# A macaron layer in split float32: a fourth seven-product pair and a fourth DMA-made second part in every feed-forward group, and the final x turned during the last products

## The chip, the cores and the metric

The kernel runs on one core of one Trainium2 chip. The metric is the device time of one execution in microseconds; lower is better.

## The reference

One layer on x (256 tokens of 2048 features) with a memory of 256 tokens: a half-weighted SwiGLU feed-forward, a mixer of a convolution branch and a spatially gated branch, cross-attention into the memory with four heads, a second half-weighted SwiGLU feed-forward, and a last normalisation over features. The two feed-forwards are what the change touches:

```python
D_MODEL = 2048; SEQ = 256; D_FF = 5632

def swiglu_ffn(h, w_in, w_out):
    gate, up = jnp.split(h @ w_in, 2, axis=-1)
    return (jax.nn.silu(gate) * up) @ w_out

h = rms_norm(x, ffn1_norm);  x = x + 0.5 * swiglu_ffn(h, ffn1_w_in, ffn1_w_out)
...                                    # mixers, cross-attention
h = rms_norm(x, ffn2_norm);  x = x + 0.5 * swiglu_ffn(h, ffn2_w_in, ffn2_w_out)
return rms_norm(x, final_norm)
```

All inputs are float32, and the precision of float32 is kept by splitting every operand into two parts (below).

## The kernel before

**Products in two parts.** TensorE multiplies in a type with fewer bits than float32 (`F32R`). Each weight tile of 128 x 1024 is therefore split into a first part (ScalarE casts it, L341 in the feed-forward's first layer and L112 elsewhere) and a second part, what the cast left out (VectorE subtracts, L342 and L113). x is split likewise. A product is three matmuls: first by first, first by second, second by first. Weights stream from HBM on SyncE's queue, 512 KB a tile, each read once.

**The first layer of a feed-forward** (class `FeedForward`) runs over 11 groups of 512 hidden features. A group's weights are 2048 rows (16 tiles of 128, index k) by 1024 columns (512 gate, 512 up). Group 0 is done plainly in `run`. Groups 1 to 10 are done by `group`, which takes the 16 tiles as 8 pairs p (k = 2p and 2p+1) after a pattern of letters:

- `C` (`eight`): two tiles of 12 matmuls each, 24 in all (`by_two`, L288 to L291: L288 is first by first, L289 reads the weight's second part, L291 reads the first part again). Work besides: a cast and a subtraction for each tile.
- `S` (`seven`): the pair, both halves of the tokens and both of the columns are taken as a 2 x 2 block matrix, and seven products of sums stand for eight, 21 matmuls in all (`three`, L275 to L277). Work besides: four additions of 128 x 512 on VectorE (L387, L388, L393, L400), three casts and subtractions of 128 x 1024 and one of 128 x 512. The sums of x that it needs (`sides`) are made once, during group 0.

After the last `S` pair VectorE combines four accumulators (L439 to L442), after the last `C` pair it adds the rest (L452), and ScalarE and VectorE make the hidden features (L417, L419).

**Second parts by DMA** (`summed`, L354 to L359). For the tiles listed in `SUMMED`, all in `C` pairs, VectorE does not subtract. ScalarE writes the negated cast into the second half of the buffer `hl_s` (L357) and the cast into the first half (L358), and GpSimd's queue then issues a DMA that adds the raw tile onto the negated half (L359). There is one buffer `hl_s`. So a turnaround is: the last matmul that reads its second part (an L289), then L357, then the DMA of L359, then the first L289 of the next summed tile. The raw tile stays held until the DMA has read it.

**Order.** A scheduling layer sets the order of each engine's instructions at build time by its own costs; on the chip each engine then runs its list in that order, waiting on semaphores. Parts go through five buffers in turn (three `hl`, two `ring`), raw tiles through four buffers `raw` and a few pieces of the tile `spare`. In the first feed-forward those pieces are five (nine raw buffers in all). In the second the first 4096 columns of `spare` hold `x2`, the final x with tokens on partitions; 32 pieces of work (`turn`, L978, one transpose of 32 x 512 each) fill it, spread by `put` and `beside` over group 0 and the groups after. Until `x_turned` in group 3 there is one extra piece of `spare` (five raw buffers); then the tile `xT` is given up for four more (`raws`).

**The second layer** (`gemm_n`, L160 to L177): four blocks of 512 columns, 22 steps of two weight tiles each, 24 matmuls a step. After a block `add_up` adds it to `x2`.

Of the kernel before, what the change touches and what calls it, by code (L numbers as in the profile page):

```python
# [11 lines left out]
F32 = mybir.dt.float32  # L12
# [5 lines left out]
P = 128  # L18
D = 2048
# [16 lines left out]

PATTERNS = ("SCSCSCCC", "SCSCSCCC")

SUMMED = (2, 7, 13)

# [26 lines left out]
def layer(ctx: ExitStack, tc: tile.TileContext, a: dict):  # L67
    nc = tc.nc
    out = a["out"]
# [18 lines left out]
    def put(cost, *parts):  # L88

        later.extend((cost, p) for p in parts)  # L90
# [9 lines left out]
    def finish():  # L100
        while later:
            later.popleft()[1]()
# [196 lines left out]
    class FeedForward:  # L299
# [6 lines left out]
        def __init__(self, stack, tags, x_hl, gain, w_in, pattern):  # L306
# [18 lines left out]
            self.sums = spare[:, 4096:5120]  # L325
            self.raws = [spare[:, 5120:6144]]
            if tags[0] == "S1":
                self.raws += [spare[:, i * 1024:(i + 1) * 1024] for i in range(4)]
            self.raw_at = 0
# [92 lines left out]

        def group(self, j, r, per, after=()):
            b = {}
# [9 lines left out]
            for p, c in enumerate(self.pattern):  # L434
# [8 lines left out]
                else:  # L443
                    late = p > self.spairs[-1] and len(after) > 0
                    self.eight(j, p, b, p == self.pattern.index("C"), p == n - 1, late)
                    if p > self.spairs[-1] + 1:
                        for _ in range(2):
                            if after:
                                after.pop(0)()
                beside(per)  # L450
            for acc, u in (("2", p1), ("4", u2), ("3", u4), ("8", u5)):
                nc.vector.tensor_tensor(out=u, in0=u, in1=b[acc], op=ALU.add)  # L452
            self.give(j, (p1, u2), (u4, u5), r)

        def run(self, before, after, root, then, per):
            acc = token_accs()
# [13 lines left out]
            for j in range(1, NG):  # L470
                if j == 3:
                    then()
                if j < NG - 1:
                    self.group(j, r, per)
                else:
                    now, turns = turns[:4], turns[4:]
                    self.group(j, r, per, now)
            return turns
# [46 lines left out]
    with ExitStack() as stack:  # L525
# [21 lines left out]

        turns = ff.run(x_arrives, x_more, x_root, lambda: None, 0.0)

# [419 lines left out]
    with ExitStack() as stack:  # L969
        ff = FeedForward(stack, ("S0", "S1", "S2"), x_hl, "ffn2_norm", a["ffn2_w_in"], PATTERNS[1])  # L970
        x2 = ff.x2

        def turn(i, j):

            def go():
                q = j % 4
                dst = x2[32 * q:32 * q + 32, j // 4].rearrange("p (f n) -> p f n", n=P)
                nc.vector.transpose(  # L978
                    out=dst[:, :, 32 * i:32 * i + 32], in_=xT[32 * i:32 * i + 32, :, 32 * j:32 * j + 32]
                )  # L980
            return go

        h = ff.of
        put(0.6, *[turn(i, j) for i in range(4) for j in range(8)])

        def first_beside(k):
            if k in (6, 9, 12):
# [51 lines left out]
        for n in range(3):  # L1039
            acc = gemm_n(a["ffn2_w_out"][n], h) if n else acc_0  # L1040
            for t in range(2):
                add_up(t, slice(n * 512, (n + 1) * 512), acc[t], n)


# [92 lines left out]
```

## Time and profile before

| what | value |
|---|---|
| time, median of 3 runs | 2136.71 us (2135.22 to 2139.54) |
| the profiled execution's own time | 2133.17 us |
| its span, first to last instruction | 2131.4 us |
| TensorE busy | 2091.1 us (98%), 9764 matmuls |
| VectorE busy | 1559.3 us (73%) |
| ScalarE busy | 1153.5 us (54%) |
| DMA read from HBM | 405.99 MB |

TensorE's busy share is modelled at the ends of matmuls, so what counts is the idle time between matmuls and who ended it. A "summed" DMA is one issued at L359. Windows below are us from the start of the span: groups 1 to 10 of the first feed-forward run from about 54 to 437, the second's from about 1435 to 1874.

### The profile page before, as it was taken

Reading aid. Unit: us, or ns where it says so; the run is one execution under the profiler, and the core shown is the slowest. Engines: PE = TensorE matmul, PEld = TensorE weight load, DVE = VectorE, ACT = ScalarE, POOL = GpSimd, SP = SyncE. Lnnn points to the kernel's source line nnn. Section 1 sums busy time; section 2 is a strip of 40 time slices with the busy share of each in tenths; the row PEclk is TensorE's granted clock in tenths of the full one; section 3 lists DMA queues with packets and bytes.
Section 4 is the critical chain, followed back from the end, with each engine's and each line's share of the span. In section 5 each row is a group of like instructions: output and inputs, shape, how many; then the busy total and the mean of one; then the engine's idle time right before and its main releaser. Section 6 shows DMA issues by size and latency. Waiting matters only on the chain. (4 is left out here: it accounts for less than half of the span.)

```text
span 2131.4 us, 26548 instructions
## 1 busy us (share of the span) xinstructions
PE 2091.1 (98%) x9764; PEld 1739.2 (82%) x9764; DVE 1559.3 (73%) x2119; ACT 1153.5 (54%) x1450; POOL 63.9 (3%) x81
## 2 busy tenths in 40 slices
PE   8999999999999999999999999998999999999998
PEld 6887888888888888888888888886788778888886
DVE  6887888776655589888877666797777888765444
ACT  7655566555544454445754455554565566554443
POOL 0000000000000000000000000000000000000000
PEclk9999999999999999999999999999999999999999
DMA  9787778855766766666655544566788778656664
GB/s 349 218 240 227 240 236 242 254 159 169 220 191 188 222 223 201 180 186 180 187 193 185 185 153 129 192 201 195 238 242 236 232 233 257 188 157 203 191 194 149
DMA packets 121954, 440.23 MB, mean 207 GB/s; under 512 B 13664, under 2 KB 13792, under 8 KB 121696
## 3 DMA queue, kind: packets, MB, share of 16 engines
q1 hardware_dynamic: 113184, 407.35, 59.6%
q0 software_dynamic: 8352, 30.41, 7.7%
q8 instruction: 76, 1.25, 0.2%
q10 hardware_dynamic: 288, 0.79, 0.1%
q14 instruction: 54, 0.44, 0.1%
HBM read 405.99 MB, written 2.10 MB: 191 GB/s over the span
## 5 line engine op out<-in xcount | busy, mean ns | idle before, releaser
L113 DVE TENSOR_TENSOR hl<-raw,hl 128x1024 fp32r<-128x1024 f32 (+1 forms) x402 | 489.8, 1219 | 322.1 <-ACT hl L112 321.2
L112 ACT CAST hl<-raw 128x1024 fp32r<-128x1024 f32 (+1 forms) x402 | 419.5, 1045 | 485.9 <-PE acc L173 299.7
L288 PE MATMUL acc<-hl,x_hl 128*128 128x512 f32 x440 | 151.6, 395 | 15.1 <-ACT hl L341 15.1
L341 ACT CAST hl<-spare 128x1024 fp32r<-128x1024 f32 (+1 forms) x105 | 102.8, 999 | 107.5 <-DVE spare L388 69.3
L342 DVE TENSOR_TENSOR hl<-raw,hl 128x1024 fp32r<-128x1024 f32 (+1 forms) x115 | 130.2, 1137 | 40.1 <-ACT hl L341 39.7
L289 PE MATMUL acc<-hl,x_hl 128*128 128x512 f32 x440 | 158.3, 395 | 0.1
L341 ACT CAST hl<-raw 128x1024 fp32r<-128x1024 f32 (+1 forms) x115 | 111.3, 981 | 71.6 <-DVE raw L400 40.8
L291 PE MATMUL acc<-hl,x_hl 128*128 128x512 f32 x440 | 137.9, 393 | 0.0
L342 DVE TENSOR_TENSOR hl<-spare,hl 128x1024 fp32r<-128x1024 f32 (+1 forms) x105 | 120.7, 1159 | 21.2 <-ACT hl L341 21.0
L341 ACT CAST ring<-spare 128x1024 fp32r<-128x1024 f32 (+1 forms) x75 | 74.1, 996 | 68.7 <-DVE spare L388 43.5
L288 PEld LDWEIGHTS acc<-hl,x_hl 128*128 128x128 f32 x440 | 83.5, 191 | 33.2 <-ACT hl L341 15.9
L172 PE MATMUL acc<-hl,x_hl 128*128 128x512 f32 x256 | 100.5, 392 | 0.1
L172 PE MATMUL acc<-hl,m_hl 128*128 128x512 f32 x256 | 100.3, 392 | 0.0
L173 PE MATMUL acc<-hl,m_hl 128*128 128x512 f32 x256 | 100.2, 391 | 0.0
L173 PE MATMUL acc<-hl,x_hl 128*128 128x512 f32 x256 | 99.8, 390 | 0.0
L289 PEld LDWEIGHTS acc<-hl,x_hl 128*128 128x128 f32 x440 | 83.3, 190 | 18.6 <-DVE hl L342 1.5
L291 PEld LDWEIGHTS acc<-hl,x_hl 128*128 128x128 f32 x440 | 83.7, 190 | 17.7
L342 DVE TENSOR_TENSOR ring<-spare,ring 128x1024 fp32r<-128x1024 f32 (+1 forms) x75 | 86.3, 1156 | 11.4 <-ACT ring L341 11.4
L289 PE MATMUL acc<-ring,x_hl 128*128 128x512 f32 x256 | 92.0, 390 | 2.1 <-DVE ring L342 2.1
L289 PE MATMUL acc<-hl_s,x_hl 128*128 128x512 f32 x232 | 89.3, 390 | 2.2 <-DMA hl_s<-raw 1.7
L171 PE MATMUL acc<-hl,m_hl 128*128 128x512 f32 x256 | 91.2, 392 | 0.0
L125 PE MATMUL acc<-x_hl,hl 128*128 128x512 f32 x256 | 91.0, 398 | 0.0
(343 smaller groups left out, 5185.4 us busy)
## 6 DMA issues: line engine op xcount, KB each, us to landing
raw<-in_ffn_w_in SPq DMA_DIRECT2D x176, 512.0 KB, 4.8
raw<-in_ffn_w_out SPq DMA_DIRECT2D x176, 512.0 KB, 3.8
spare<-in_ffn_w_in SPq DMA_DIRECT2D x120, 512.0 KB, 5.1
raws<-in_ffn_w_in SPq DMA_DIRECT2D x56, 512.0 KB, 5.1
raw<-in_w_mix_vg SPq DMA_DIRECT2D x32, 512.0 KB, 4.6
raw<-in_w_k SPq DMA_DIRECT2D x32, 512.0 KB, 3.9
raw<-in_w_v SPq DMA_DIRECT2D x32, 512.0 KB, 4.3
raw<-in_w_mix_out SPq DMA_DIRECT2D x32, 512.0 KB, 3.8
```

Source lines behind the costliest of these rows:

```text
L112: nc.scalar.copy(out=hl[:, 0, :size], in_=raw[:, :size])
L113: newest[0] = nc.vector.tensor_tensor(out=hl[:, 1, :size], in0=raw[:, :size], in1=hl[:, 0, :size].bitcast(F32), op=ALU.subtract)
L125: nc.tensor.matmul(acc, lhsT=w_hi, rhs=x_hl, start=first, stop=False, skip_group_check=True)
L171: nc.tensor.matmul(acc[t], lhsT=x[:, 0, s], rhs=hi[:, k], start=k0 + k == 0, stop=False)
L172: nc.tensor.matmul(acc[t], lhsT=x[:, 0, s], rhs=lo[:, k], start=False, stop=False)
L173: nc.tensor.matmul(acc[t], lhsT=x[:, 1, s], rhs=hi[:, k], start=False, stop=k0 + k == nk - 1)
L288: nc.tensor.matmul(acc[t][g], lhsT=x[:, 0, s], rhs=hi[:, cols[g]], start=(t, g) in first, stop=False)
L289: nc.tensor.matmul(acc[t][g], lhsT=x[:, 0, s], rhs=lo[:, cols[g]], start=False, stop=False)
L291: nc.tensor.matmul(acc[t][g], lhsT=x[:, 1, s], rhs=hi[:, cols[g]], start=False, stop=last)
L341: nc.scalar.copy(out=hl[:, 0, :n], in_=raw[:, :n])
L342: newest[0] = nc.vector.tensor_tensor(out=hl[:, 1, :n], in0=raw[:, :n], in1=hl[:, 0, :n].bitcast(F32), op=ALU.subtract)
```

## The change

Three things are changed.

1. The pattern of both feed-forwards becomes `SCSCSSCC`: four `S` pairs of 8 a group, two of them (p = 4 and 5) next to each other. `sides` makes a fourth set of sums, at k = 15 of group 0.
2. `SUMMED` becomes (2, 6, 12, 15): four tiles a group have their second part made by DMA. The buffer `hl_s` stays one.
3. The 32 transposes of the final x leave the second feed-forward's groups. They become 128 transposes of 32 x 128 (L973), 32 of them beside block 0 of the last products and 96 beside blocks 1 and 2. `xT` is kept to the end, and both feed-forwards have nine raw buffers from the start, five of them in `spare`.

```diff
-PATTERNS = ("SCSCSCCC", "SCSCSCCC")
-
-SUMMED = (2, 7, 13)
+PATTERNS = ("SCSCSSCC", "SCSCSSCC")
+
+SUMMED = (2, 6, 12, 15)
...
-            self.raws = [spare[:, 5120:6144]]
-            if tags[0] == "S1":
-                self.raws += [spare[:, i * 1024:(i + 1) * 1024] for i in range(4)]
+            self.raws = [spare[:, i * 1024:(i + 1) * 1024] for i in (5, 0, 1, 2, 3)]
...
-                    if p > self.spairs[-1] + 1:
+                    if p >= n - 2:
...
-                beside(per)
...
-                if j == 3:
-                    then()
...
-            if k in (6, 9, 12):
+            if k in (6, 9, 12, 15):
                 ff.sides(k // 3 - 2)
-            beside(0.8)
-
-        def x_turned():
-            finish()
-            raws = xt.tile([P, 4, 1024], F32, name="raws", tag="x")
-            ff.raws += [raws[:, i] for i in range(4)]
-
-        turns = ff.run(lambda k: None, first_beside, lambda: rms_cols(ss, D, "r_x2"), x_turned, 0.6)
+        turns = ff.run(lambda k: None, first_beside, lambda: rms_cols(ss, D, "r_x2"))
+        put(0.3, *[turn(0, i, j) for i in range(4) for j in range(8)])
+        acc_0 = gemm_n(a["ffn2_w_out"][0], h, per=0.55, between=turns, after=0)
         finish()
-        acc_0 = gemm_n(a["ffn2_w_out"][0], h, between=turns, after=0)
...
         for n in range(3):
-            acc = gemm_n(a["ffn2_w_out"][n], h) if n else acc_0
+            if n == 1:
+                put(0.3, *[turn(m, i, j) for m in range(1, 4) for i in range(4) for j in range(8)])
+            acc = gemm_n(a["ffn2_w_out"][n], h, per=0.75) if n else acc_0
```

The lines above keep their meaning in the changed kernel but move: L357 and L359 become L355 and L357, L341 and L342 become L339 and L340; L275 to L291 stay.

**Where the order changes: TensorE around the summed tiles.** The names in a row are accumulator, weights and x, and what it waits for; the landing of a summed DMA is awaited as `DMASW`. Before, ahead of one of a group's three summed tiles in the first feed-forward. The second part of the summed tile before it was read for the last time 43 matmuls earlier; these are the last rows of that stretch:

```order
L277 MATMUL acc<-ring 128x512
L275 MATMUL aux<-hl,ring 128x512 [waits Activation_49]
L276 MATMUL aux<-hl,ring 128x512 [waits DVE_49]
L277 MATMUL aux<-hl,ring 128x512
L275 MATMUL acc<-hl,x_hl 128x512 [waits DVE_49,Activation_49]
L276 MATMUL acc<-hl,x_hl 128x512
L277 MATMUL acc<-hl,x_hl 128x512
L288 MATMUL acc<-hl_s,x_hl 128x512 [waits Activation_49]
L289 MATMUL acc<-hl_s,x_hl 128x512 [waits DMASW6_49]
```

Now, between a group's tile 15 and the next group's tile 2. The first row shown is the fifth matmul after the last that reads the second part of tile 15; the last row reads that of tile 2:

```order
L276 MATMUL acc<-ring,x_hl 128x512
L277 MATMUL acc<-ring,x_hl 128x512
L275 MATMUL acc<-ring 128x512 [waits DVE_49]
L276 MATMUL acc<-ring 128x512
L277 MATMUL acc<-ring 128x512
L275 MATMUL acc<-ring,x_hl 128x512 [waits DVE_49,Activation_49]
L276 MATMUL acc<-ring,x_hl 128x512
L277 MATMUL acc<-ring,x_hl 128x512
L288 MATMUL acc<-hl_s,x_hl 128x512 [waits Activation_49]
L288 MATMUL acc<-hl_s,x_hl 128x512 x2
L288 MATMUL acc<-hl_s,x_hl 128x512 [waits DVE_49]
L289 MATMUL acc<-hl_s,x_hl 128x512 [waits DMASW0_49]
```

So this turnaround has 16 matmuls from the start of one L289 to the start of the other, where the one before had 43. Over both feed-forwards the order before has 56 turnarounds, none under 34 matmuls and most of 43 to 61. The changed order has 76; 36 of them have 16 to 28 matmuls, 20.6 on average (tile 12 to 15, and 15 to the next 2), and the other 40 have 30 to 45.

**ScalarE, first feed-forward.** Before, between two negated casts:

```order
L357 ACTIVATE hl_s<-spare 128x1024 [waits DMAHW0_49,DMASW6_49,PE_49]
L358 CAST hl_s<-spare 128x1024 [waits PE_49,Activation_49]
L341 CAST hl<-raw 128x512 [waits DVE_49,Activation_49]
L341 CAST ring<-raw 128x1024 [waits DMAHW5_49,PE_49,Activation_49]
L341 CAST ring<-spare 128x1024 [waits PE_49,Activation_49]
L341 CAST hl<-raw 128x1024 [waits DMAHW0_49,PE_49,Activation_49]
L341 CAST hl<-spare 128x1024 [waits DMAHW7_49,PE_49,Activation_49]
L341 CAST hl<-spare 128x512 [waits DVE_49,PE_49,Activation_49]
L341 CAST ring<-spare 128x1024 [waits DMAHW1_49,PE_49,Activation_49]
L357 ACTIVATE hl_s<-raw 128x1024 [waits DMAHW6_49,DMASW7_49,PE_49]
```

Now, three negated casts (for tiles 15, 2 and 6) within twelve rows:

```order
L355 ACTIVATE hl_s<-spare 128x1024 [waits DMASW2_49,PE_49]
L356 CAST hl_s<-spare 128x1024 [waits PE_49]
L339 CAST hl<-spare 128x1024 [waits DMAHW3_49,PE_49]
L339 CAST ring<-raw 128x512 [waits DVE_49]
L355 ACTIVATE hl_s<-raw 128x1024 [waits DMAHW5_49,DMASW3_49,PE_49]
L415 ACTIVATE h_109<-spare,r_x_95 128x512 [waits DVE_49]
L356 CAST hl_s<-raw 128x1024 [waits PE_49,Activation_49]
L415 ACTIVATE h_109<-spare,r_x_95 128x512 [waits DVE_49]
L339 CAST ring<-spare 128x1024 [waits DMAHW0_49,PE_49]
L339 CAST hl<-spare 128x1024 [waits DVE_49]
L339 CAST hl<-spare 128x1024 [waits DMAHW5_49,DVE_49]
L355 ACTIVATE hl_s<-spare 128x1024 [waits DMASW4_49,PE_49]
```

Two of the three casts to come are now a few rows apart, and each of them waits for TensorE's last read of `hl_s`.

**VectorE, the transposes.** Before, in group 0 of the second feed-forward, between the subtractions of weights:

```order
L342 TENSOR_TENSOR hl<-raw,hl 128x1024
L978 STREAM_TRANSPOSE spare<-xT 32x16x32 x2
L342 TENSOR_TENSOR ring<-spare,ring 128x1024
L978 STREAM_TRANSPOSE spare<-xT 32x16x32
L342 TENSOR_TENSOR hl<-raw,hl 128x1024
```

Now, in block 1 of the last products:

```order
L113 TENSOR_TENSOR hl<-raw,hl 128x1024
L973 STREAM_TRANSPOSE spare<-xT 32x4x32 x3
L113 TENSOR_TENSOR hl<-raw,hl 128x1024
L973 STREAM_TRANSPOSE spare<-xT 32x4x32 x2
L113 TENSOR_TENSOR hl<-raw,hl 128x1024
```

They stand behind a subtraction as before, two or three of a quarter of the size.

More of the change, by code (lines that the diff above doesn't have):

```diff
@@ L421, in give, with group @@
                 )
-        def group(self, j, r, per, after=()):
+        def group(self, j, r, after=()):
             b = {}
@@ L453, in group, with run @@
             self.give(j, (p1, u2), (u4, u5), r)
-        def run(self, before, after, root, then, per):
+        def run(self, before, after, root):
             acc = token_accs()
@@ L470, in run @@
             for j in range(1, NG):
-                if j == 3:
-                    then()
                 if j < NG - 1:
-                    self.group(j, r, per)
+                    self.group(j, r)
                 else:
                     now, turns = turns[:4], turns[4:]
-                    self.group(j, r, per, now)
+                    self.group(j, r, now)
             return turns
@@ L546, in x_root @@
             return r_x
-        turns = ff.run(x_arrives, x_more, x_root, lambda: None, 0.0)
+        turns = ff.run(x_arrives, x_more, x_root)
         sm = st.tile([P, T], F32, name="sm")
```

11 lines of the change are left out of this document (6 added, 5 removed).

## The prediction

> **What bounds the kernel now.** I read the engines' busy times first, then stretches of time that hold whole groups, then who ended TensorE's waits. All times are of one profiled execution, 2133.17 us with a span of 2131.4; the median of the three runs, 2136.71, is 3.5 us more. From the page's first part, then the table of stretches (us of a stretch, then busy us and instructions of TensorE, its weight loads, VectorE, ScalarE, GpSimd, then granted clock, DMA share, GB/s), then TensorE's waits (total, times, longest; the last row those between 1433 and 1537 alone):
>
> ```profile
> PE 2091.1 (98%) x9764; PEld 1739.2 (82%) x9764; DVE 1559.3 (73%) x2119; ACT 1153.5 (54%) x1450; POOL 63.9 (3%) x81
> ...
> 97.80:393.30 295.50, 291.07 (x1280) 239.48 (x1279) 239.12 (x289) 175.39 (x196) 18.23 (x21) 1.00 0.79 237
> 1433.00:1485.00 52.00, 44.44 (x184) 35.41 (x183) 39.54 (x48) 25.48 (x30) 2.61 (x3) 0.90 0.63 179
> 1485.00:1537.00 52.00, 47.51 (x201) 38.34 (x200) 40.72 (x51) 27.49 (x32) 2.62 (x3) 0.97 0.78 236
> 1996.00:2056.00 60.00, 60.00 (x266) 49.69 (x266) 28.92 (x24) 24.68 (x27) 2.97 (x2) 1.00 0.65 193
> ...
> PE acc L288 <- ACT hl L341: 15.1, 3, 7.4
> PE acc L275 <- DVE spare L452: 6.3, 6, 1.5
> PE acc L275 <- ACT hl L341: 3.2, 3, 2.6
> PE acc L289 <- DVE ring L342: 2.1, 2, 1.4
> PE acc L289 <- DMA hl_s<-raw: 1.7, 1, 1.7
> ...
> PE acc L288 <- ACT hl L341: 7.2, 1, 7.2
> ```
>
> TensorE is the bound: 98% busy, and its five largest kinds of waits on other engines come to 28.4 us. The stretch 1996 to 2056 has it busy throughout: 266 matmuls in 60 us, 0.226 us each. The stretch 97.8 to 393.3 is seven groups of the first feed-forward, 42.2 us each; a group's 183 matmuls by 0.226 are 41.4, so 0.8 us a group is waiting. VectorE is busy 239.12 / 7 = 34.2 us of a group, ScalarE 25. The second feed-forward's first two `S` groups take 104 us for two, 19.6 more than twice 42.2: with five raw buffers and the transposes, TensorE waits there for casts, once 7.2 us, and the granted clock falls to 0.90 and 0.97.
>
> **Fewer matmuls.** One more `S` pair in each of 20 groups takes 3 matmuls each: 60 x 0.226 = 13.6 us less on the bounding engine.
>
> **More work on VectorE and ScalarE.**
>
> ```profile
> L342 DVE TENSOR_TENSOR hl<-raw,hl 128x1024 fp32r<-128x1024 f32 x97 | 117.8, 1220 | 27.8 <-ACT hl L341 27.4
> L342 DVE TENSOR_TENSOR hl<-raw,hl 128x512 fp32r<-128x512 f32 x18 | 12.5, 692 | 12.4 <-ACT hl L341 12.4
> L387 DVE TENSOR_TENSOR spare<-raw 128x512 f32<-128x512 f32 x30 | 20.6, 686 | 23.7 <-DMA raw<-in_ffn_w_in 23.7
> L978 DVE STREAM_TRANSPOSE spare<-xT 32x512 f32<-32x512 f32 x32 | 22.5, 703 | 0.8
> ...
> L341 ACT CAST hl<-raw 128x1024 fp32r<-128x1024 f32 x97 | 100.6, 1048 | 28.7 <-PE acc L291 10.2 <-DMA raw<-in_ffn_w_in 7.3 <-issue 4.3
> ```
>
> An `S` pair costs VectorE 4 x 0.686 + 3 x 1.220 + 0.692 = 7.1 us, a `C` pair 2.44, so the exchange adds 4.7; one more summed tile takes 1.2 back. A group's VectorE work becomes 34.2 + 3.5 = 37.7 us against 180 x 0.226 = 40.7 us of matmuls, 93%. It still fits, and the five buffers let VectorE run ahead wherever TensorE waits for something else, so I add nothing; the price if it doesn't fit is a rival below. ScalarE gets a cast and a half and one of the two of a summed tile more, about 2.7 us by 1.048 each, and stays under 28: nothing. The fourth `sides` stands in group 0, where VectorE has no pairs to add for: nothing, at worst its few operations of 0.7 us, 3 us in each feed-forward.
>
> **Transposes moved.** 32 of 0.703 us leave the second feed-forward, and nine raw buffers stand from the start, as in the first. I take the early groups' excess as gone: 19.6 us less, at least 12 if part of it is the start of the pipeline. The 128 small ones are not in this trace. By area one costs 0.703 / 4 = 0.18, by count 0.70 at most, so 23 to 90 us over three blocks of the last products. A block has 28.92 of 60 us of VectorE, and even 30 more leaves it inside TensorE's 60. They stand behind subtractions that run ahead, so zero; if their cover fails, a few us.
>
> **The turnaround of `hl_s`.** This decides. The first three rows are one turnaround in order of time (start, duration); the last two are landing times of L359's DMA (min, median, max), of all 58 and of the one at 287.2:
>
> ```profile
> 217.91 0.39 PE L289 MATMUL acc<-hl_s,x_hl 128*128 128x512 f32 x1
> ...
> 218.34 1.06 ACT L357 ACTIVATE hl_s<-spare 128x1024 fp32r<-128x1024 f32 x1 [1.21 <-PE acc L289]
> ...
> 219.80 0.87 POOL L359 DMA_DIRECT2D hl_s<-spare  x1 [15.41 <-ACT hl_s L357]
> ...
> DMA to landing us min/median/max: 4.5/4.8/9.0
> ...
> DMA to landing us min/median/max: 8.8/8.8/8.8
> ```
>
> From the last L289 to the negated cast is 0.43 us, from there to the DMA 1.46, and to the landing 4.5 at least, 4.8 at the median, 9.0 at most. A turnaround thus takes 6.4, 6.7 or up to 10.9 us. Before, the shortest holds 34 matmuls, 7.7 us, and most 43 or more, 9.7 us, so that the median is covered everywhere, and TensorE waited 1.7 us once. In the changed order 36 turnarounds hold 20.6 matmuls on average, 4.66 us. TensorE runs in order and cannot pass the L289 that waits. Each costs 6.7 - 4.66 = 2.04 us at the median, 73 us in all; at the minimum 62. A quarter to a third of the landings collide with loads, like the one at 287.2; at about 8 instead of 4.8 for one in three the sum is 73 + 12 x 3.2 = 111. While TensorE waits, no raw buffer comes free and fewer loads start, so I take one in six: 92 us. The 40 longer turnarounds (30 to 45 matmuls, 6.8 to 10.2 us) are covered at the median and I add nothing. The waits at a group's end (6.3 us on L452) lie within the turnaround from tile 15 to the next 2, and vanish in it: 6.3 less.
>
> **The clock.** A wait can also slow what follows:
>
> ```profile
> 1510.79 0.50 PE L275 MATMUL acc<-hl,ring 128*128 128x512 f32 x1 [2.58 <-ACT hl L341]
> ...
> 1511.00:1515.00 4.00, 3.83 (x10) 2.80 (x10) 4.00 (x4) 3.31 (x4) 0.00 (x0) 0.57 0.62 119
> ```
>
> After a wait of 2.58 us the granted clock was 0.57 for 4 us: 10 matmuls where 17 or 18 would fit, 1.7 us lost. The shortest turnarounds (16 to 18 matmuls, half of the 36) leave 2.6 to 3.1 us of waiting at the median, just there. I take six such losses, 10 us; none to all 36 (61 us) is possible. The Trainium skill, "TensorE: Matmul & The Clock Gate", section "Part 1: The HAM clock gate", says that the clock falls to half after an idle window of about 3.4 us that runs freely, and comes back after as long a time of work; the row shows the fall after less. By that rule most waits here would keep the clock, and only collided landings would lose it, which puts the sum some 10 us lower or leaves it.
>
> **Sum.** -13.6 (matmuls) - 19.6 (early groups) - 6.3 (group ends) + 92 (turnarounds) + 10 (clock) = +62.5. 2133.2 + 62.5 = 2195.7, against the median 2199. I predict 2198.
>
> **Rivals.**
> - *The transfers are hidden and it gets faster.* Then 39.5 us go and 2094 is left (2097 by the median). The break-even is a turnaround of 4.66 + 39.5 / 36 = 5.76 us, a landing 3.9 us after the issue. No landing of the trace is under 4.5, and only the order of the instructions could make room. The Trainium skill, "DMA: Bandwidth & Descriptors", section "Anatomy of one DMA", fits 2.0 us plus the bytes by 436 GB/s for a DMA of GpSimd's queue: an estimate of 3.2 us for 512 KB. By it a turnaround would take 5.1 us, the sum would be -39.5 + 16 = -23, and the kernel would be faster, at about 2113; the trace's 4.5 to 9.0 speaks against it. Chance 0.07.
> - *VectorE becomes the bound.* Today it idles 42.2 - 34.2 = 8 us a group, mostly waiting for casts. If the 8 us stay, a group takes 45.7: 18 x 3.5 - 2 x 6.3 = +50, 2187. For it speaks the 93%; against it that it runs ahead. The waits would then be on subtractions and not on the DMA. Chance 0.08.
> - *The clock falls after nearly every wait.* 51 us more than I took and collisions at one in three: 2198 + 51 + 19 = 2268. Chance 0.10.
> - *Gain and loss cancel* within 0.2% (about what a measurement of this kernel can tell from no change): the waits would have to come to 40 us, less than their minimum. Chance 0.03.
>
> **How the numbers follow.** My forecast, slower by the turnarounds with part of the clock, has 0.72. Its range: at the low end every landing at its minimum, no clock loss: -39.5 + 62 = +22, 2159 by the median. At the high end one in three collides, the early groups give back 12, and the clock takes 30: -32 + 111 + 30 = +109, 2246. The VectorE rival lies inside. The range 2156 to 2248 leaves out the faster rival, the cancelling one and the clock at its worst, 0.2 together. Faster 0.07, same 0.03, slower 0.90.
>
> **What would show it.** TensorE's waits of L289 on the landing of `hl_s` become its largest, 70 to 110 us over about 36 to 50 waits, nearly all ahead of tiles 15 and 2. A group of the first feed-forward takes 44 to 47 us with TensorE's clock under 1.00 in the stretch, while VectorE's busy time grows to 37 or 38. The second feed-forward's groups look like the first's, with no wait of 7 us for a cast. The last products keep 60 us a block. I am wrong if landings come sooner than 4.5 us, if the turnaround is shorter than 6.4, or if TensorE's waits are on VectorE.

## The result, and the profile after

| | before | after |
|---|---|---|
| median us (lowest to highest) | 2137.20 (2135.22 to 2139.54) | 2260.49 (2256.66 to 2267.61) |
| ratio to before, 95% interval | | 1.058 (1.0552 to 1.0609) |
| span of the profiled execution, us | 2131.4 | 2258.6 |
| first `S` matmul of group 1 to last matmul of group 10, first feed-forward, us | 421.3 | 485.6 |
| the same, second feed-forward, us | 438.5 | 501.0 |

The kernel is 5.8% slower: 123 us, where 61 were forecast, and above the forecast's range. The two stretches of groups grew by 64.4 and 62.5 us, 126.9 of the 127.2 us by which the span grew. Everything else kept its time. (Before, the first of them runs from 55.0 to 476.2 us of the span, not to 437 as "Time and profile before" has it.) The page's first part, after:

```profile
PE 2132.5 (94%) x9704; PEld 1749.6 (77%) x9704; DVE 1645.3 (73%) x2325; ACT 1213.7 (54%) x1516; POOL 83.7 (4%) x101
```

Two stretches of groups and one of the last products (columns as in the prediction):

```profile
54.00:520.00 466.00, 416.04 (x1718) 331.02 (x1717) 357.23 (x438) 268.14 (x297) 32.56 (x38) 0.95 0.74 211
1500.00:1985.00 485.00, 428.54 (x1734) 338.75 (x1733) 357.46 (x437) 267.13 (x296) 32.91 (x38) 0.94 0.72 202
2123.00:2183.00 60.00, 60.00 (x267) 49.67 (x266) 41.46 (x68) 24.57 (x26) 4.29 (x2) 1.00 0.66 193
```

In the groups TensorE is busy 88 to 89% of the time and its granted clock is 0.94 to 0.95; in the last products it has 60.00 of 60 us, though VectorE's load there rose from 28.92 to 41.46 us with the transposes. TensorE's longest waits (total, times, longest), and the landing times of the summed DMA:

```profile
PE acc L289 <- DMA hl_s<-spare: 60.6, 23, 6.7
PE acc L289 <- DMA hl_s<-raw: 32.0, 15, 5.8
PE acc L288 <- ACT hl L339: 8.5, 2, 6.7
PE acc L275 <- ACT hl L339: 6.9, 4, 2.6
PE acc L276 <- DVE hl L340: 3.1, 3, 1.9
...
DMA to landing us min/median/max: 4.5/5.7/8.7
```

38 waits for a landing come to 92.6 us; no wait on VectorE comes near. (6.7 us of the L288 row is the kernel's first matmul.) One of them in order of time (start, duration, at the end the idle time): the last L289 of one summed tile, a cast of another tile, the negated cast of the next summed tile, its DMA, the L289 that waits for it; then the stretches of the wait and of the 4 us behind it.

```profile
241.19 0.39 PE L289 MATMUL acc<-hl_s,x_hl 128*128 128x512 f32 x1
...
241.67 1.05 ACT L339 CAST ring<-raw 128x1024 fp32r<-128x1024 f32 x1
242.62 1.05 ACT L355 ACTIVATE hl_s<-spare 128x1024 fp32r<-128x1024 f32 x1
...
244.07 0.87 POOL L357 DMA_DIRECT2D hl_s<-spare  x1 [20.76 <-ACT hl_s L355]
...
251.62 1.22 PE L289 MATMUL acc<-hl_s,x_hl 128*128 128x512 f32 x2 [5.77 <-DMA hl_s<-spare]
```

```profile
245.00:252.00 7.00, 1.23 (x5) 0.75 (x4) 0.69 (x1) 0.60 (x1) 0.00 (x0) 0.82 0.99 275
252.00:256.00 4.00, 4.00 (x10) 3.09 (x10) 2.27 (x4) 1.41 (x2) 0.00 (x0) 0.50 0.46 138
```

The turnaround took 10.4 us, 3.7 more than the forecast's median. ScalarE began the negated cast 1.43 us after the last L289 and not 0.43, because the other cast ran; and the landing took 7.5 us (to 251.6) instead of 4.8. Three loads of 512 KB were issued from 243.05 us on, just ahead of it, and the DMA engines were 0.99 busy; that these loads made the landing long is likely, but no run separates it. Behind the wait 10 matmuls took 4 us at a clock of 0.50.

The two stretches together, worked out from the starts of their matmuls. What counts is the time from one start to the next, less the 0.2265 us of a matmul at full clock:

| part | forecast | measured |
|---|---|---|
| 60 matmuls fewer | -13.6 | -13.6 |
| waits for landings, starts over 0.6 us apart | +92 | +96.4 |
| other starts over 0.6 us apart | -25.9 | -6.5 |
| matmuls at half the clock (0.36 to 0.5 us apart) | +10 | +33.6 |
| the rest: short losses (starts mostly 0.25 to 0.36 and 0.5 to 0.6 us apart) | none | +17.0 |
| sum | +62.5 | +126.9 |

### The profile page after: what moved, and what is told of

It is laid out like the page before. It is cut to its first block, busy times and chain, and to the rows that moved or that the text cites. A ratio compares the mean times of both kernels' runs of the same rounds, so it can differ in the third digit from the quotient of the medians.

```text
span 2258.6 us, 26762 instructions
## 1 busy us (share of the span) xinstructions
PE 2132.5 (94%) x9704; PEld 1749.6 (77%) x9704; DVE 1645.3 (73%) x2325; ACT 1213.7 (54%) x1516; POOL 83.7 (4%) x101
## 4 chain that ended last, share of the span: by engine, by line
PE 56%; issue 38%; DMA 3%; POOL 2%; DVE 1%; ACT 1%; POOLq 0%; SPq 0%; DVEq 0%; ACTq 0%
PE acc L172 11%; PE acc L173 11%; PE acc L171 11%; PE acc L125 8%; PE acc L126 4%; POOL hl_s L357 2%; PE acc L289 2%; PE acc L291 1%; PE acc L288 1%; PE aux L263 1%; DMA raw<-in_ffn_w_in 1%; PE acc L1049 1%; PE acc L1050 1%; DMA hl_s<-spare 1%; PE acc L1051 1%
## 5 line engine op out<-in xcount | busy, mean ns | idle before, releaser
L113 DVE TENSOR_TENSOR hl<-raw,hl 128x1024 fp32r<-128x1024 f32 (+1 forms) x402 | 489.0, 1217 | 283.1 <-ACT hl L112 282.1
L112 ACT CAST hl<-raw 128x1024 fp32r<-128x1024 f32 (+1 forms) x402 | 419.6, 1045 | 486.5 <-PE acc L173 295.5
L340 DVE TENSOR_TENSOR hl<-spare,hl 128x1024 fp32r<-128x1024 f32 x176 | 214.0, 1222 | 35.4 <-ACT hl L339 34.7
L339 ACT CAST hl<-spare 128x1024 fp32r<-128x1024 f32 x176 | 182.7, 1050 | 99.6 <-PE aux L277 38.0
L289 PE MATMUL acc<-hl_s,x_hl 128*128 128x512 f32 x312 | 123.3, 455 | 93.0 <-DMA hl_s<-spare 60.6
L289 PEld LDWEIGHTS acc<-hl_s,x_hl 128*128 128x128 f32 x312 | 62.6, 212 | 122.9 <-DMA hl_s<-spare 71.7
L339 ACT CAST hl<-raw 128x1024 fp32r<-128x1024 f32 x88 | 92.4, 1051 | 87.5 <-PE aux L277 56.7
L288 PE MATMUL acc<-hl,x_hl 128*128 128x512 f32 x336 | 125.0, 405 | 8.5 <-ACT hl L339 8.5
L289 PE MATMUL acc<-hl,x_hl 128*128 128x512 f32 x336 | 129.2, 406 | 0.1
L340 DVE TENSOR_TENSOR hl<-raw,hl 128x1024 fp32r<-128x1024 f32 x88 | 107.4, 1222 | 27.5 <-ACT hl L339 25.8
L291 PE MATMUL acc<-hl_s,x_hl 128*128 128x512 f32 x312 | 114.9, 442 | 0.0
L291 PE MATMUL acc<-hl,x_hl 128*128 128x512 f32 x336 | 109.1, 397 | 0.0
L339 ACT CAST ring<-spare 128x1024 fp32r<-128x1024 f32 (+1 forms) x96 | 81.6, 850 | 48.9 <-DVE spare L398 18.4
L340 DVE TENSOR_TENSOR ring<-spare,ring 128x1024 fp32r<-128x1024 f32 (+1 forms) x96 | 93.8, 977 | 16.1 <-ACT ring L339 15.9
L355 ACT ACTIVATE hl_s<-spare 128x1024 fp32r<-128x1024 f32 x44 | 46.6, 1058 | 104.2 <-PE acc L289 81.9
L288 PE MATMUL acc<-hl_s,x_hl 128*128 128x512 f32 x312 | 100.0, 396 | 2.3 <-ACT hl_s L356 0.6
L172 PE MATMUL acc<-hl,x_hl 128*128 128x512 f32 x256 | 100.4, 392 | 0.2 <-DVE hl L113 0.2
L173 PE MATMUL acc<-hl,x_hl 128*128 128x512 f32 x256 | 99.8, 390 | 0.0
L449 DVE TENSOR_TENSOR spare<-spare,acc 128x512 f32<-128x512 f32 x80 | 50.9, 683 | 63.8 <-PE acc L291 63.8
```

Source lines behind the costliest of these rows:

```text
L112: nc.scalar.copy(out=hl[:, 0, :size], in_=raw[:, :size])
L113: newest[0] = nc.vector.tensor_tensor(out=hl[:, 1, :size], in0=raw[:, :size], in1=hl[:, 0, :size].bitcast(F32), op=ALU.subtract)
L172: nc.tensor.matmul(acc[t], lhsT=x[:, 0, s], rhs=lo[:, k], start=False, stop=False)
L173: nc.tensor.matmul(acc[t], lhsT=x[:, 1, s], rhs=hi[:, k], start=False, stop=k0 + k == nk - 1)
L288: nc.tensor.matmul(acc[t][g], lhsT=x[:, 0, s], rhs=hi[:, cols[g]], start=(t, g) in first, stop=False)
L289: nc.tensor.matmul(acc[t][g], lhsT=x[:, 0, s], rhs=lo[:, cols[g]], start=False, stop=False)
```

## The experiments

Eighteen kernels. In the table "pairs" are the `S` pairs of a group, "raw" the raw buffers; then the median, its ratio to before in the same session (95% interval), TensorE's waits for landings (us, times), and what both feed-forwards' groups lose, in us: under "clock" at half the clock (starts 0.36 to 0.5 us apart), under "gaps" at all other starts over 0.25 us apart. Between sessions the median of the kernel before moved from 2129.3 to 2137.2 us, so a difference in us between kernels of two sessions is good to some 8 us; the ratios take this out. From e5 on, but for e6, lines L339 and L340 are L341 and L342; in e16 L449 is L456 and the second addition of an `S` pair, L386, is L393.

| kernel | pairs, pattern | summed | `hl_s` | raw | us | ratio | landings | gaps | clock |
|---|---|---|---|---|---|---|---|---|---|
| before | 3 SCSCSCCC | 2, 7, 13 | 1 | 5, then 9 | 2137.2 | | 2.1, 2 | 26 | 3 |
| after | 4 SCSCSSCC | 2, 6, 12, 15 | 1 | 9 | 2260.5 | 1.058 (1.0552-1.0609) | 92.6, 38 | 131 | 36 |
| e1 | 3 SCSCSCCC | 2, 7, 13 | 1 | 9 | 2114.6 | 0.990 (0.9887-0.992) | 0 | 10 | 0 |
| e2 | 4 SCSCSSCC | 2, 7, 13 | 1 | 9 | 2178.1 | 1.021 (1.0185-1.0231) | 9.3, 4 | 69 | 18 |
| e3 | 3 SCSCSCCC | 2, 6, 12, 15 | 1 | 9 | 2188.5 | 1.026 (1.0244-1.0275) | 18.5, 18 | 71 | 9 |
| e4 | 4 SCSCSCSC | 2, 6, 10, 14 | 1 | 9 | 2216.3 | 1.038 (1.0361-1.0406) | 65.3, 38 | 92 | 18 |
| e5 | 4 SCSCSSCC | 2, 6, 12, 15 | 2 | 7 | 2247.3 | 1.053 (1.0501-1.0561) | 11.7, 12 | 143 | 17 |
| e6 | 3 SCSCSCCC | 2, 7, 13 | 1 | 7 | 2173.1 | 1.019 (1.0166-1.0213) | 5.0, 7 | 57 | 11 |
| e7 | 4 SCSCSSCC | 2, 7, 13 | 2 | 7 | 2223.1 | 1.042 (1.0393-1.0455) | 0 | 110 | 26 |
| e8 | 3 SCSCSCCC | 2, 6, 12, 15 | 2 | 7 | 2185.9 | 1.024 (1.0217-1.027) | 1.3, 2 | 64 | 18 |
| e9 | 4 SCSCSSCC | 2, 6, 12, 15 | 2 | 9 | 2197.9 | 1.030 (1.0281-1.0318) | 27.4, 18 | 84 | 21 |
| e10 | 4 SCSCSSCC | 2, 7, 13 | 1 | 11 | 2132.3 | 0.999 (0.9978-0.9998) | 6.4, 6 | 35 | 7 |
| e11 | 4 SCSCSSCC | 2, 6, 12, 15 | 1 | 11 | 2250.8 | 1.054 (1.0526-1.056) | 96.0, 50 | 122 | 38 |
| e12 | 4 SCSCSSCC | 2, 7, 13 | 2 | 9 | 2147.5 | 1.006 (1.0045-1.0084) | 0 | 43 | 6 |
| e13 | 3 SCSCSCCC | 2, 7, 13 | 1 | 11 | 2106.8 | 0.989 (0.9872-0.9905) | 0 | 1 | 0 |
| e14 | 3 SCSCSCCC | 2, 6, 12, 15 | 1 | 11 | 2173.6 | 1.021 (1.0186-1.0233) | 48.4, 30 | 62 | 9 |
| e15 | 4 SCSCSCSC | 3, 7, 14 | 1 | 11 | 2131.5 | 1.000 (0.9996-1.0015) | 12.1, 12 | 33 | 1 |
| e16 | 4 SCSCSCSC | 2, 6, 10, 14 | 2 | 9 | 2134.2 | 1.002 (1.0003-1.0026) | 0 | 30 | 5 |
| e17 | 4 SCSSCSCC | 3, 8, 12, 15 | 2 | 9 | 2125.6 | 0.998 (0.997-0.9995) | 5.5, 5 | 28 | 5 |
| e18 | 4 SSCSCSCC | 4, 8, 12, 14 | 2 | 9 | 2131.9 | 1.001 (0.9998-1.0016) | 6.0, 10 | 36 | 2 |

### The parts of the change one by one: e1, e2, e3

```diff
e1  -PATTERNS = ("SCSCSSCC", "SCSCSSCC")     +PATTERNS = ("SCSCSCCC", "SCSCSCCC")
    -SUMMED = (2, 6, 12, 15)                 +SUMMED = (2, 7, 13)
    -            if k in (6, 9, 12, 15):     +            if k in (6, 9, 12):
e2  -SUMMED = (2, 6, 12, 15)                 +SUMMED = (2, 7, 13)
e3  -PATTERNS = ("SCSCSSCC", "SCSCSSCC")     +PATTERNS = ("SCSCSCCC", "SCSCSCCC")
    -            if k in (6, 9, 12, 15):     +            if k in (6, 9, 12):
```

> Only the third part of the change: pattern SCSCSCCC and summed tiles 2, 7, 13 as before, the 32 transposes out of the second feed-forward's groups and nine raw buffers there from the start. Turnaround theory: the second feed-forward's groups lose their excess over the first's (438.5 - 421.3 = 17 us from start to end of groups 1 to 10), nothing else moves, 2113 to 2125 us; no wait of L289 on a landing. Rival (the moved transposes or the held xT cost what the change lost): 2160 or more, with the loss behind 1860 us.

> Four seven-product pairs, three summed tiles a group (2, 7, 13); order has 56 turnarounds again, the shortest 30 matmuls, most 36 to 51. Turnaround theory: the waits for landings go (under 10 us in sum), the clock stays at 0.99 to 1.00 in the groups, and the time is 2137 - 13.6 - 17 = 2106 us, with some waits for casts or second parts 2100 to 2125. VectorE theory: VectorE has one subtraction a group more than in the changed kernel, about 38.9 us of a group of 40.7 us, and every delay behind it costs: 2140 to 2190 us, with waits on L340 and on the additions L385 to L398.

> Three seven-product pairs as before, four summed tiles a group (2, 6, 12, 15); 76 turnarounds, 18 of 24 to 28 matmuls (26 on average), the next at 32. Chain 7.6 us (0.43 + 1.46 + a landing of 5.7) against 26 x 0.2265 = 5.9 us. Turnaround theory: 18 to 20 waits of 1.7 us, 15 to 32 us in sum, and 5 to 10 us of clock behind them, less 17 us of the moved transposes: 2137 - 17 + 24 + 8 = 2152 us (2130 to 2170), faster than the changed kernel though it has all its summed tiles. VectorE theory: a subtraction a group less than before makes it 2110 to 2120. Theory that each summed transfer costs whatever the distance (traffic, a held raw buffer): 20 more than before, half of the loss at least, 2180 or more.

The third part alone gains 20 us, the prediction's 19.6, and its two feed-forwards now take 421.7 and 419.6 us. The other two parts were a surprise. On top of e1 the fourth pair alone costs 64 us and the fourth summed tile, with the places that go with it, alone 74; together they cost about 145. The time of e2 lies in the range of the VectorE theory and that of e3 in the range of a price for each transfer; e10 and e16 below speak against both. In e2 only 9.3 us are waits for a landing, so the turnaround theory cannot account for it. TensorE's waits, then those of SyncE's queue, e1 ahead of e2:

```profile
PE acc L275 <- DVE spare L449: 7.1, 6, 2.1
...
SPq L349 <- DMA hl_s<-spare: 64.7, 24, 6.8
SPq L349 <- DMA hl_s<-raw: 61.6, 25, 6.4
```

```profile
PE acc L275 <- ACT hl L339: 12.4, 10, 4.7
PE acc L289 <- DMA hl_s<-raw: 9.3, 4, 2.8
PE acc L276 <- DVE hl L340: 5.7, 6, 2.5
...
SPq L349 <- DMA hl_s<-spare: 173.7, 31, 9.7
SPq L349 <- DMA hl_s<-raw: 155.9, 26, 12.4
```

A load of L349 needs a free raw buffer, and the buffers go round in a fixed order. With as many summed tiles, the queue of loads stood 330 us instead of 126 behind a raw tile that a summed DMA still had to read. That time alone is no loss: e16 and e17 below stand 346 and 354 us in these rows and lose little. It costs where the load then comes too late. One such case of e2, from the queue to TensorE:

```profile
303.03 0.33 SPq L349 DMA_DIRECT2D spare<-in_ffn_w_in  x1
...
304.99 0.86 POOL L357 DMA_DIRECT2D hl_s<-spare  x1 [10.23 <-ACT hl_s L355]
...
311.49 0.33 SPq L349 DMA_DIRECT2D spare<-in_ffn_w_in  x1
...
315.14 0.69 DVE L385 TENSOR_TENSOR spare<-spare 128x512 f32<-128x512 f32 x1 [2.47 <-DMA spare<-in_ffn_w_in]
...
317.64 0.80 PE L275 MATMUL acc<-hl,ring 128*128 128x512 f32 x1 [4.66 <-ACT hl L339]
```

The summed DMA of 304.99 lands after 6.4 us, at 311.4; only then can the next load go, for which VectorE's first addition of an `S` pair waits, for that a cast, and for that TensorE. Its wait is written down to ScalarE; the held raw buffer is four steps back. Of the 54 us that e2 loses at starts over 0.6 us apart, 28 to 31 go over a summed landing ahead of a load when each wait is followed back like this, 25 or 40 us far.

### Distance: e4

```diff
-PATTERNS = ("SCSCSSCC", "SCSCSSCC")
-SUMMED = (2, 6, 12, 15)
+PATTERNS = ("SCSCSCSC", "SCSCSCSC")
+SUMMED = (2, 6, 10, 14)
...
-                    if p >= n - 2:
-                        for _ in range(2):
+                    if p == n - 1:
+                        for _ in range(4):
```

> As many seven-product pairs and summed tiles as in the changed kernel, but at equal distances: pattern SCSCSCSC, summed tiles 2, 6, 10, 14. 76 turnarounds, 20 under 30 matmuls (25 on average), 32 more of 30 to 33. With a chain of 6.7 us the waits come to 21 us in sum, with 7.6 us to 55 us. Turnaround theory: 2137 - 13.6 - 17 + 38 + 12 of clock = 2156 us (2125 to 2185), about 100 under the changed kernel. VectorE theory and theory of a price for each summed transfer: the same work a group, so 2240 or more.

Even distances win 44 us, not 100. Waits for landings remain the largest:

```profile
PE acc L289 <- DMA hl_s<-raw: 41.3, 20, 3.3
PE acc L289 <- DMA hl_s<-spare: 24.0, 18, 2.6
```

The sum of one loop says why. Paired row by row in the changed kernel's trace, a landing comes 7.9 us (median) after the start of the last L289 of the tile before, not 6.7, and from the start of a tile's first L289 to that of its last 1.8 us pass. Four loops of 9.7 are 39 us of a group's 40.7 us of matmuls; three loops are 29 of 41.4. With four summed tiles the one buffer is as good as full, and even spacing could not save more than e4 did: any delay of a load or a cast becomes a wait.

### Raw buffers: e6, e10, e11, e13, e14

Seven buffers leave two pieces of `spare` out. Eleven need 8 KB a partition: the hidden features of group 10 go to `sums`, those of group 9 to a raw piece, which the last group then does without (ten there).

```diff
e6 (on e1)             -for i in (5, 0, 1, 2, 3)]   +for i in (5, 0, 2)]
e10, e11, e13, e14     -for j in range(NG)]         +for j in range(NG - 2)]
    +self.h += [spare[:, c:c + 1024].rearrange("p (t n) -> p t n", t=2) for c in (3072, 4096)]
    +self.raws[:0] = [self.own.tile([P, 1024], F32, name=f"raw{i}") for i in range(2)]
```

> The third part of the change alone (2114 us) with seven raw buffers instead of nine; pattern, summed tiles and the one hl_s as before the change. Theory that the raw ring is the limit as soon as it is shorter or held longer: a load is issued two tiles later, 5 us at 2.6 us a tile, so stalls as in the kernel with four seven-product pairs and three summed tiles (54 us), 2140 to 2180 us. Theory of the single buffer's turnaround alone: shortest turnaround 30 matmuls, nothing changes, 2114 to 2122.

> Four seven-product pairs, three summed tiles, one hl_s, eleven raw buffers instead of nine (ten in the last group); with nine it was 2178 us. Shortest turnaround 31 matmuls. Raw ring theory: two more buffers are worth what two fewer cost in the kernel with three pairs (59 us), up to the whole of its stalls (54 us and 18 of clock): 2105 to 2130 us. VectorE theory (38.9 of 40.7 us a group): 2165 to 2185, waits on L340 and the additions without a load behind them.

> The changed kernel with eleven raw buffers and its one hl_s. Order has 36 turnarounds under 30 matmuls, 25.2 on average, and 30 more of 30 to 34. Turnaround theory: raw buffers do not help a landing that is late by its own chain; waits on landings stay at 36 us (chain of 6.7 us) to 83 us (7.6 us) with the clock's loss, 2160 to 2240. Raw ring theory: 2120 or less.

> The third part of the change alone (three seven-product pairs, three summed tiles, 2114 us) with eleven raw buffers instead of nine. Shortest turnaround 46 matmuls. Its groups take 841 us against 833 us of matmuls, so at most 8 us are there to be won: raw ring theory 2106 to 2113, every other theory 2114.

> Three seven-product pairs, four summed tiles (2, 6, 12, 15), one hl_s, eleven raw buffers; with nine 2188 us. 18 turnarounds of 25 to 28 matmuls as with nine. Raw ring theory: what goes back over a load (27 us of its stalls, and the clock behind them) goes, the waits on landings (21 us) stay, 2140 to 2160. Turnaround theory alone: no change, 2180 to 2190.

Two buffers fewer cost e1 about 60 us (e6): 47 in gaps, most of them in waits for casts and second parts, and 11 at half the clock:

```profile
PE acc L275 <- ACT hl L339: 8.3, 7, 2.9
PE acc L289 <- DVE ring L340: 5.6, 5, 2.7
PE acc L289 <- DVE hl L340: 4.8, 7, 1.4
```

Two more win e2 46 us (e10; SyncE's queue stands 237 us instead of 330 behind summed tiles), 2 us over the range I gave, though VectorE has as much to do as in e2 and a subtraction a group more than in the changed kernel. So VectorE was not what held e2; of the 64 us that the fourth pair costs with nine raw buffers, two more give 46 back. In e13 the groups stand for nothing: the stretch that the prediction showed of before has 1304 matmuls where 1280 were, and the largest wait left is that of the kernel's first matmul:

```profile
97.80:393.30 295.50, 295.43 (x1304) 244.31 (x1303) 242.79 (x291) 182.25 (x200) 18.23 (x21) 1.00 0.79 239
...
PE acc L288 <- ACT hl L341: 7.6, 1, 7.6
```

In the changed kernel itself two more buffers win only 10 us (e11, 11 over its range), and in e3 only 15 (e14, a miss by 13 us at the least; by the ratios 8 and 11): the waits behind loads go, and waits for landings take their place, in e14 18.5 us with nine buffers and now

```profile
PE acc L289 <- DMA hl_s<-raw: 28.3, 18, 3.1
PE acc L289 <- DMA hl_s<-spare: 20.1, 12, 3.1
```

So with one `hl_s` there are two limits side by side: the raw buffers for the fourth pair, the one `hl_s` for the fourth summed tile. The profile names the one that ends last.

### A second `hl_s`: e5, e7, e8, e9, e12

```diff
+self.hls = [self.hl, self.own.tile([P, 2, 1024], F32R, name="hl_t")]
...
-w = self.parts(self.raw(j, k), last=plain) if at is False else self.hl
+w = self.parts(self.raw(j, k), last=plain) if at is False else self.hls[at % 2]
e5, e7, e8: two raw buffers fewer, and the tile after the next asked for behind the matmuls
-    self.summed(*self.sums_at[at + 1])      +    self.summed(*self.sums_at[at + 2])
e9, e12: room made as in e10, and the next tile asked for ahead of by_two
```

> The changed kernel with a second hl_s buffer: the negated cast of a summed tile no longer waits for the last matmul on the summed tile before it, but for the one before that. Its 8 KB a partition come from two raw buffers (seven instead of nine; the last two groups' hidden features lie in the final x's place). Distances in the order: 74 turnarounds, 4 under 30 matmuls, 14 under 34, most of 46 to 83. Theory of the single buffer (both the short turnaround and the raw tile that it holds back): waits on landings fall from 93 us to under 15, and the clock's loss with them; 2137 - 13.6 - 17 + 10 = 2116 us (2095 to 2150). Rival (the ring of raw buffers and the queue of loads are the limit, whoever holds them): two raw buffers fewer make it no better than the changed kernel, 2200 or more, with waits behind loads. Rival VectorE: 2190 as in the prediction.

> Four seven-product pairs, three summed tiles (2, 7, 13), two hl_s buffers and seven raw buffers; with one buffer and nine raw buffers it was 2178 us, and 30 of 54 us of its stalls go back over a load that waited for a raw tile held by a summed transfer. Theory that the hold is the cause: the raw tile is freed as soon as its own cast and transfer are done, stalls under 20 us, 2105 to 2130. VectorE theory (38.9 of 40.7 us a group): it stays at 2160 to 2190, with waits on L340 and the additions. Raw ring theory: 2180 or more.

> Three seven-product pairs, four summed tiles (2, 6, 12, 15), two hl_s buffers and seven raw buffers; with one buffer and nine raw buffers it was 2188 us. Shortest turnaround 38 matmuls. Theory of the single buffer: no waits on landings, 2114 to 2130. Theory that each summed transfer costs, by traffic: 2160 or more. Raw ring theory: 2180 or more.

> The changed kernel with a second hl_s buffer and all nine raw buffers (eight in the last group): the 8 KB come from the hidden features of the last two groups, which lie in a raw piece and in the tile sums. The next summed tile is asked for just before the matmuls on the present one. The clean form of the experiment that took two raw buffers (2247 us). Distances: 74, 4 under 30 matmuls, 16 under 34. Theory of the single buffer: waits on landings under 15 us (93 in the changed kernel), the clock's loss under 10, and no raw tile held for a free hl_s: 2095 to 2125 us. Theory that loads are the limit with nine raw buffers too, once four pairs a group take two raw tiles at a time: the waits come back behind loads, 2160 to 2200.

> Four seven-product pairs, three summed tiles, two hl_s buffers, nine raw buffers (eight in the last group); with one hl_s and nine it was 2178, with two and seven 2223 us. Theory that a raw tile is held for a free hl_s: the second buffer frees it early, 2105 to 2140. Raw ring theory: nine are too few for four pairs, whoever holds them, 2165 to 2190. VectorE theory: the same 2165 to 2185, but with no load behind the waits.

e5 shows both limits at once: waits for landings fall from 92.6 to 11.7 us, as expected, and the time only from 2260 to 2247, as the rival of the raw buffers had it, since seven of them bring new waits:

```profile
PE acc L275 <- ACT ring L341: 25.1, 15, 3.6
PE acc L288 <- ACT hl L341: 22.5, 10, 7.6
PE acc L276 <- DVE hl L342: 20.3, 19, 2.5
```

With nine (e9) it is 2198. That is 62 us under the changed kernel and not the 135 to 165 of the single-buffer theory; the range of the loads theory, 2160 to 2200, holds it. 27.4 us for landings are left, and 31 us in the second of the two adjacent pairs, all of them behind a load when followed back:

```profile
PE aux L276 <- DVE hl L342: 31.3, 14, 4.0
PE acc L289 <- DMA hl_s<-spare: 16.7, 8, 3.3
PE acc L289 <- DMA hl_s<-raw: 10.7, 10, 1.5
```

The three-summed kernel goes the same way: 2178 with one `hl_s` and nine buffers, 2223 with two and seven (e7), 2147.5 with two and nine (e12, a little over its range). e8 stayed at 2186, where hardly a landing was waited for. For e7 and e8 the expectation of the hold was wrong and that of the raw buffers right. Between e5 and e9, and between e7 and e12, the place at which a summed tile is asked for changed as well as the buffers; how much each did was not separated. Nor does the second `hl_s` make the fourth summed tile free: in this pattern, with nine raw buffers, it still costs 50 us (e12 to e9).

### Whether four pairs can pay: e15, e16, e17, e18

e15 is e10 and e16 to e18 are e9 with the patterns and summed tiles of the table; e15 and e16 also have the last edit of e4.

> Four seven-product pairs a group, each followed by a plain one (SCSCSCSC), three summed tiles (3, 7, 14), one hl_s, eleven raw buffers; with SCSSCC and 2, 7, 13 it was 2132 us. VectorE has 14.0 us of work in two adjacent seven-product pairs, which are 9.5 us of matmuls, and 9.4 us in a seven-product and a plain pair with a summed tile, which are 10.2. Theory that adjacent pairs are what is left of the stalls: 2105 to 2125. VectorE theory (38.9 of 40.7 us a group, whatever the order): 2130 or more.

> As many seven-product pairs and summed tiles as in the changed kernel (four and four), but SCSCSCSC and 2, 6, 10, 14, a second hl_s and nine raw buffers. Shortest turnaround 37 matmuls. With the changed kernel's order the second hl_s and nine raw buffers took 2198 us, its waits before the second of two adjacent pairs behind loads. Theory of the two mechanisms (hl_s and raw buffers): both have room now, 2100 to 2125 us, waits on landings under 5 us, the clock falls fewer than 5 times. If the summed transfers cost by traffic or in another way: 2150 or more.

> The kernel with SCSCSCSC, four summed tiles, a second hl_s and nine raw buffers (2134 us), but SCSSCSCC and summed tiles 3, 8, 12, 15: two adjacent pairs in the middle, two plain pairs at the group's end. Shortest turnaround 53 matmuls. Theory that the group's end is what was left: the waits on the additions at the end (21 us) go, 2100 to 2118 us. Theory that two adjacent pairs cost in loads as they did with SCSSCC (2198 us): 2140 or more.

> The same with SSCSCSCC and summed tiles 4, 8, 12, 14: the two adjacent pairs stand at the group's start, behind the two plain pairs of the group before it, in which ScalarE and VectorE have the least work. Shortest turnaround 40 matmuls. Theory that the group's end is what was left: 2100 to 2118 us. Theory of adjacent pairs: 2140 or more, with waits on the second pair's casts and second parts behind loads.

e16 does all the matmuls, pairs and transfers of the changed kernel, without a wait for a landing, 5 us of clock, and 126 us less. So the transfers by themselves cost at most what is left here. It is 9 us over its range all the same, since it waits at the group's end instead, for VectorE's additions there (totals first, then one such wait in order of time):

```profile
PE acc L275 <- DVE spare L456: 15.7, 9, 4.4
...
PE aux L275 <- DVE spare L446: 5.2, 12, 0.8
...
439.98 0.69 DVE L393 TENSOR_TENSOR spare<-spare 128x512 f32<-128x512 f32 x1 [4.79 <-DMA spare<-in_ffn_w_in]
...
441.18 0.68 DVE L456 TENSOR_TENSOR spare<-spare,acc 128x512 f32<-128x512 f32 x1
...
442.01 0.77 PE L275 MATMUL acc<-hl,x_hl 128*128 128x512 f32 x1 [4.40 <-DVE spare L456]
```

The wait is written down to VectorE, but VectorE itself had stood idle 4.79 us for a load, ahead of an addition of an `S` pair. So it was at all nine waits on L456: at most 3.2 us ahead of each, VectorE had stood 0.3 to 4.8 us for a load. What is left in e16 begins with loads too.

e17 wins some 7 us of those 21 by the ratios and e18 2, both less than expected. But e17 and e18 have two adjacent pairs as e9 has, and take 72 and 66 us less. So adjacent pairs alone are not what e9 lost by; the places of the summed tiles changed with the pattern (shortest turnaround 53 and 40 matmuls, in e9 four under 30), and the two were not separated. e15, with three summed tiles and so more work for VectorE, came out where the VectorE theory put it (2130 or more), but its trace does not bear that theory out: 12.1 us of its waits are for landings, and of some 10 us for second parts, 8 come behind an addition for which VectorE had itself stood idle for a load. None of the four comes under 2125: the 13.6 us of a fourth pair go into some 30 us of remaining gaps, of which e13, with three pairs, has 1. The traces point at loads that come late; whether more raw buffers would cure that, with a second `hl_s` and even spacing together, was not tried, and which resource would have to grow for a fourth pair to pay stays open. e13, at 2106.8 us, is faster than both kernels, than the one before by 1.1%.

## Why the prediction was right or wrong

- **Matmuls, transposes, the third part: right.** 60 matmuls fewer; e1 gained 20 us where 19.6 was put down; the last products kept 60 us a block.
- **The turnaround of `hl_s`: right in kind, its size partly luck.** 92.6 us in 38 waits against 92 in 36 to 50, and 33 of the 36 short turnarounds made TensorE wait. The single turnaround was longer than said: at the short ones 8.1 us on average instead of 6.7 at the median, for ScalarE was sometimes a cast late, and 11 of the 36 landings took over 6.5 us, one in three and not the one in six that was taken because "fewer loads start". In the wait shown the next load did start only at the landing (251.60), but three issued just before were still under way. At 8.1 us the 36 would have cost some 124 us; they cost 94, since delays elsewhere lengthened the distances.
- **The clock: the term that failed most, 10 forecast, 33.6 measured.** The price of a loss held: 20 losses in the groups, 1.7 us each forecast and 1.7 to 1.8 measured. The count did not, six against 20: I saw that the shortest turnarounds, half of the 36, leave 2.6 to 3.1 us of waiting, and still took six without a reason. The waits came out longer, up to 6.7 us, and the clock fell after every one of 3 us and more. The 17 us of short losses had no term at all. The rival of a clock that falls after nearly every wait (2268) was nearer the time than the forecast, but the clock fell at about half of them.
- **The credits: -25.9 forecast, -6.5 measured.** The waits on L452 at a group's end went as forecast. "The early groups' excess is gone" is true alone (e1): the 7-us wait for a cast in the second feed-forward went. Together with the rest, casts and second parts were waited for elsewhere, L275 and L276 for 11 us.
- **"It still fits, I add nothing": the step that failed in kind.** VectorE did nearly fit with four summed tiles: e16 has the same work for it and 126 us less, so the VectorE rival, as I priced it, fell. But the fourth pair does not only need VectorE, it takes two raw tiles at once and holds them through its chain of additions. That it costs 64 us alone with nine raw buffers (e2), 46 of which two more buffers give back (e10), was in none of my terms or rivals. In the changed kernel most of it seems to hide under the waits for landings: its trace hardly shows it, and e9, with 65 us less of those waits, has 31 us of waits in the added pair.
- **The miss of 64 us in the two stretches, added up:** 24 of clock, 19 of credits that did not come, 17 of short losses, 4 of landings.
- **Range.** Its high end, +109, had 111 us for the waits and 30 for the clock, enough for both; it lacked the 17 us of short losses and still counted on 18 us of credits, of which 6.5 came.

## What to carry to other kernels

A buffer that several tiles use in turn is a serial engine: add up its loop (last read, rewrite, transfer, first to last read), multiply by the uses per stage and compare with the stage; here it was full at 95%, and even spacing (e4) left 65 us of waits. When a change lengthens how long any input buffer is held, ask which load stands behind it in its queue, and follow a wait on a cast or an addition back several steps before blaming the engine that did it. How long a queue stands is not yet a loss. And test the parts of a change one by one: of two limits side by side the profile shows only the one that ends last.

## What the runs showed of the hardware

In every trace here the falls of the granted clock in the groups begin on one grid of 3.41 us, which lies elsewhere in each run but runs through the whole of it, and each lasts one to three of its steps. Whether it falls goes with how many matmuls start in the step just before; at full clock 15 fit. Of the steps at full clock in the groups of all 20 kernels, the clock fell after all 106 with 4 starts or fewer, after 37 of 111 with 5 to 7, and after none of 4835 with 8 or more. So TensorE need not be idle for a whole step, and the same wait can cost the clock or not, as it lies in one step or across two: of the waits in the changed kernel's groups (time beyond a matmul) it fell after all 12 of 3 us and more, 4 of 5 of 2.5 to 3, 4 of 19 of 1 to 2.5 and none that was shorter and stood alone. Each fall took 5 to 13 matmuls at 0.43 us. The Trainium skill, "TensorE: Matmul & The Clock Gate", section "Part 1: The HAM clock gate", gives an idle window of about 3.4 us that runs freely. The free-running window and its length agree with the traces; that it has to be idle does not, and the runs decide.

Landings of the same 512 KB transfer took 4.5 us at best and up to 8.7 in the changed kernel. The median moved from 4.8 to 5.7 with the change, the mean stayed at 5.9, and one in three took over 6.5 us in both (19 of 58, 25 of 78); loads were under way beside the long one shown.
